# The opening's four tiles by seven products in the first feed-forward block's down product

## The chip, the cores and the metric

The kernel runs on one core of a Trainium2 chip. Times are microseconds (us) of device time for one execution. TensorE (PE in the profile) multiplies matrices, VectorE (DVE) and ScalarE (ACT) do elementwise work and read the products out of PSUM, GpSimd (POOL) and SyncE (SP) here mostly issue transfers (DMA). Each engine works through its own list of instructions in the list's order and waits on semaphores for the others.

## The reference

Two layers of an encoder over 640 rows (512 prompt rows and 8 streams of 16 rows), width 1024. Each layer is a half-step feed-forward block, a mixer (short convolution and banded attention, joined by gates), and a second half-step feed-forward block. All is float32. The part that the change touches is the first block:

```python
x = x + 0.5 * swiglu(rmsnorm(x, norm_ffn1), w_gu, w_down)     # D_MODEL 1024, D_FF 2816

def _swiglu(h, w_gu, w_down):
    gu = h @ w_gu
    g, u = jnp.split(gu, 2, axis=-1)
    return (jax.nn.silu(g) * u) @ w_down
```

## The kernel before

**Layout.** The activations are held transposed, features on the 128 partitions and the 640 rows along the free axis, so x is 8 tiles of 128x640 and the hidden layer is 22 tiles (`FT`). Each float32 operand is split into a high part (ScalarE casts it, lines 221 and 307) and a low part (VectorE subtracts, lines 222 and 312), and each product is three matmuls: high by high, high by low, low by high. One matmul streams 320 columns, half of a tile's rows.

**Two ways to multiply.** A plain product of two tiles (`multiply`, line 370) takes 6 matmuls: three for each half of the rows. The other way (`block`, line 391) takes two neighbouring tiles of weights, two of the inner dimension and the two halves of the rows as a 2x2 block product and needs 7 products where the plain way needs 8. The operands are then sums and differences, of the weights and of the activations, named `X11`, `XT5`, `XN6`, `X21`, `XT7`, `X22`, `XT4` for the seven products; the results are put together by further additions.

**Units and chunks.** `gate_up` makes one hidden tile: its u and its g by seven products, 84 matmuls over four slabs of prepared weights (`s0` to `s3`). One call of it is called a unit here. The hidden tiles are worked in chunks of `FFNS`, for the first block of layer 0 ("a0") 4, 4, 4, 4, 4 and 2. The first four tiles of "a0" are the opening: they are multiplied the plain way (`opening`, line 604) while the normalisation is still being worked out. While a chunk's units run, the chunk before is multiplied with the down weights and added to x. For a chunk that is made by seven (`by_seven`), that is two calls of `down_rows`, after the second and the third unit (`ROWS`), each over four rows of output tiles: seven products of 12 matmuls over four slabs, with x updated from PSUM by VectorE (`take`), or by staging a product through ScalarE (`stage`) into an accumulating DMA that POOL issues (`send`). For other chunks it is one slab of 8 plain tiles behind each unit (two output tiles, 48 matmuls). In "a0" the four tiles of the opening go the plain way, behind units 4, 5, 6 and 7.

**Weights.** `source` loads the raw weights (SP's queue, three buffers and a fourth) and forms their sums on VectorE (line 251: two of 512 columns for slab 1, two for slab 2); `prep` casts the high part on ScalarE and `flush` emits the low part on VectorE. There are three buffers for prepared slabs; one is read by TensorE and two lie ahead. A by-seven unit or call has slabs of 1024, 1024, 1024 and 512 columns.

**Pairs.** Two hidden tiles of a chunk form a `Pair`. Its first tile gives E (the product of g and u, a difference of its halves, and the cast and low part for `X11` and `XT5`); its second gives O (`X21`, `X22`) and, in five steps of `rest`, three combinations (lines 911 and 913), their cast and low part (`XN6`, `XT7`), and a cast and low part of 320 columns (`XT4`, here called t4). E and O have one buffer each. The steps are run at named spots of later units, by `TURNS`.

**Order.** `manual_schedule` keeps the order in which the code emits instructions. In "a0" it holds for PE, DVE and ACT until unit 6 (`free`), and from there for PE alone. What closes a unit (g by the norm, the product of g and u, the pair's part) is a `tail`, which the code runs in what follows: in the slab of the down product, at spot e1 of the next unit, or in a call of `down_rows`. A unit's three PSUM banks a, b and c are copied or added out between the products (lines 820, 833, 836 copy a and c; in unit 4, which comes first, lines 767, 777 and 786); a bank that was copied takes the next product on top, so that product waits for the copy. Four such banks go round.

**The opening's tiles.** Their tails, `parts(2)`, `parts(3)`, `parts(0)`, `parts(1)`, each a cast and a low part of 640 columns, run inside unit 4, two after its first product and two after its fourth.

Of the kernel before, what the change touches and what calls it, by code (L numbers as in the profile page):

```python
# [13 lines left out]
ALU = mybir.AluOpType  # L14
# [17 lines left out]
FT = FF // P  # L32
# [45 lines left out]
def by_seven(name, j):  # L78

    at, n = chunk_at(name, j)  # L80
    return n == 4 and at >= FFNS[name][1] and at + n < FT


def ffn_order(name):
# [93 lines left out]
def halves(t):  # L178
    return t.rearrange("p (a b) -> p a b", a=2)
# [3 lines left out]
def trunk(ctx: ExitStack, tc: tile.TileContext, xin, wst, small, pbias, samplebias, kcache, vcache,  # L183
          yout, ko, vo, co):
    nc = tc.nc
    PE, DVE, ACT, POOL, SP = nc.tensor, nc.vector, nc.scalar, nc.gpsimd, nc.sync
# [33 lines left out]
    def split(hi, lo, src):  # L220
        ACT.copy(hi, src)
        DVE.tensor_tensor(out=lo, in0=src, in1=hi.bitcast(F32), op=ALU.subtract)
# [87 lines left out]
    def flush():  # L310
        for lo, src, hi in pending:
            DVE.tensor_tensor(out=lo, in0=src, in1=hi.bitcast(F32), op=ALU.subtract)  # L312
        pending.clear()
# [16 lines left out]
    def ahead():  # L330

        source(len(ready))

    def begin():

        prep(used[0] + 2)
# [264 lines left out]
            ACT.activation(early, epst, AF.Silu)  # L601
            self.known = True

    def opening(fp, name, goff, n, put, tails):

        ACT.copy(early, epst)
        ex = Expand(fp, name, goff)
        h = []  # L610
        whi, wlo = (wp.tile([P, CH], F32R, tag=f"w{t}", name=f"w{t}0", bufs=3) for t in ("hi", "lo"))
        ready.append((whi, wlo))
        for k in range(KT):
            g = sm[:, goff + k : goff + k + 1]
            hi = hp.tile([P, T], F32R, tag="hhi", name=f"hhi{name}_{k}")
            lo = hp.tile([P, T], F32R, tag="hlo", name=f"hlo{name}_{k}")
            ACT.activation(hi, x[k], AF.Copy, scale=g)
            c = slice(k * P, (k + 2) * P)
            if k % 2 == 0:
                ACT.copy(whi[:, c], raws[0][:, c])  # L620
            DVE.scalar_tensor_tensor(out=lo, in0=x[k], scalar=g, in1=hi.bitcast(F32),
                                     op0=ALU.mult, op1=ALU.subtract)
            if k % 2 == 0:
                DVE.tensor_tensor(out=wlo[:, c], in0=raws[0][:, c], in1=whi[:, c].bitcast(F32),
                                  op=ALU.subtract)
            h.append((hi, lo))
        flush()

        made = {2: (0, 1), 3: (2, 3), 4: (4,), 5: (5, 6), 6: (7,)}
        us, gs, ps = [], [], []  # L630

        def out(i):

            j, up = divmod(i, 2)
            if not up:
                gs.append(tmp(f"g{name}_{j}"))
                if j:
                    scaled(gs[j], ps[i], ex.rho)
                    ACT.activation(gs[j], gs[j], AF.Silu)
                else:  # L640
                    ACT.copy(halves(gs[j]), two(ps[i]))
                return
            u = tmp(f"u{name}_{j}") if j > 1 else fp.tile([P, T], F32, tag="cap", name=f"u{name}_{j}", bufs=5)
            us.append(u)
            if j:
                scaled(u, ps[i], ex.rho)
                DVE.tensor_tensor(out=u, in0=u, in1=gs[j], op=ALU.mult)
            else:
                ACT.copy(halves(u), two(ps[i]))

        def begun():
            ex.total(att(f"nps{name}"))
            ex.root()
            ex.diagonal()

        at = {2: {4: begun}, 3: {1: lambda: ex.spread([att(f"nbc{name}_{a}")[:, :HT] for a in range(2)])}}
        for i in range(2 * n):
            ps.append(acc(f"po{name}_{i}"))
            product(ps[i], h, at.get(i, {}))
            if i > 1:  # L660
                out(i - 1)
            if i == 0:
                for k in range(KT):
                    ex.square(k)
                    ex.add()
                    if k == 1:
                        out(0)
                    if k == 4:
                        flush()
            if i == 1:  # L670
                continue
            if i == 3:
                g, u = gs[0], us[0]
                DVE.tensor_tensor(out=g, in0=g, in1=ex.rho, op=ALU.mult)
                ACT.activation(g, g, AF.Silu)
                DVE.tensor_tensor(out=u, in0=u, in1=ex.rho, op=ALU.mult)
            flush()
            for m in made.get(i, ()):
                ex.final(m, False)
            if i == 3:  # L680
                DVE.tensor_tensor(out=u, in0=u, in1=g, op=ALU.mult)
            if i == max(made):
                ex.rest()
        ahead()
        begin()
        out(2 * n - 1)

        def parts(j, u):
            hi = hp.tile([P, T], F32R, tag="hhi", name=f"ahi{name}_{j}")
            lo = hp.tile([P, T], F32R, tag="hlo", name=f"alo{name}_{j}")  # L690
            split(hi, lo, u)
            put(j, (hi, lo))


        for j in sorted(range(n), key=lambda j: j < 2):
            tails.append(lambda j=j: parts(j, us[j]))
        ex.rest = None
        return ex

# [40 lines left out]
        with soon():  # L740
            last(pa)

    def gate_up(fp, n, ex, first, tails, put, j, pair, later, at):

        pa, pb, pc = (att(f"p{i}{n}")[:, :HT] for i in "abc")

# [5 lines left out]

        def spot(name):
            step(later, f"g{at}{name}")

        every, most, end = range(NP), range(NP - 1), range(NP - 1, NP)
        g, u = tmp(f"g{n}"), tmp(f"u{n}")
# [59 lines left out]
        else:  # L817
# [3 lines left out]
            prep(used[0] + 1)  # L821
            spot("e1")
            for t in tails:
                t()
            tails.clear()
            spot("e2")
            flush()
# [21 lines left out]
        DVE.tensor_tensor(out=g[:, t1], in0=pa, in1=rho[:, t1], op=ALU.mult)  # L849
        ACT.activation(g, g, AF.Silu, scale=-1.0)  # L850
        spot("e7")
        flush()

        def tail(weights=True):
            if weights:
                begin()
            DVE.tensor_tensor(out=g, in0=g, in1=rho, op=ALU.mult)
            hi = hp.tile([P, T], F32R, tag="hhi", name=f"ahi{n}")
            lo = hp.tile([P, T], F32R, tag="hlo", name=f"alo{n}")
            if pair:  # L860
                pair.product(n, u, g, hi, lo)
            else:
                DVE.tensor_tensor(out=u, in0=u, in1=g, op=ALU.mult)
                flush()
                split(hi, lo, u)
            put(j, (hi, lo))
            if weights:
                ahead()

        tails.append(tail)  # L870

    class Pair:
# [8 lines left out]
        def product(self, n, u, g, hi, lo):  # L881
            if self.E is None:

                z = self.E = self.fp.tile([P, 3, HT], F32, name=f"de{n}", tag="even", bufs=1)
                DVE.tensor_tensor(out=z[:, 0:3:2], in0=halves(u), in1=halves(g), op=ALU.mult)
                DVE.tensor_tensor(out=z[:, 1], in0=z[:, 0], in1=z[:, 2], op=ALU.subtract)
                at, kinds = slice(0, 2), (X11, XT5)
            else:

                z = self.O = self.fp.tile([P, 5, HT], F32, name=f"do{n}", tag="odd", bufs=1)  # L890
                DVE.tensor_tensor(out=z[:, 3:5], in0=halves(u), in1=halves(g), op=ALU.mult)
                at, kinds = slice(3, 5), (X21, X22)
                self.later.append(self)
                self.work = self.rest()
            flush()
            ACT.copy(halves(hi), z[:, at])
            self.low(halves(lo), halves(hi), z[:, at])
            self.keep(kinds, hi, lo)

        def low(self, lo, hi, z):  # L900
            DVE.tensor_tensor(out=lo, in0=z, in1=hi.bitcast(F32), op=ALU.subtract)
# [27 lines left out]
    def step(later, place):  # L929

        for p in later:
            while p.done < 5 and p.spots[p.done] == place:
                next(p.work)
                p.done += 1
# [83 lines left out]
    def ffn(name, fp, ex, goff, after, end=False):  # L1018
# [7 lines left out]
        hold[0] = True  # L1026

        mode = ExitStack()
        free = min(j for j in range(FT) if by_seven(name, j)) + 2

        def order(engines):
            mode.close()
# [1 line left out]

        order(ORDERED)
        if plain:
            ex = opening(fp, name, goff, plain, act.__setitem__, tails)
        for what, a in ffn_order(name):
            if what == "gu" and a == free:
                order({mybir.EngineType.PE})  # L1040
# [4 lines left out]
            if what == "gu":  # L1045
                pair = None
                if by_seven(name, a):
                    i, odd = divmod(a - chunk_at(name, a)[0], 2)
                    if not odd:
                        at = chunk_at(name, a)[0]  # L1050
                        rows = at and by_seven(name, at - 1)
                        pairs[a] = Pair(fp, f"{name}_{a}", i, later, TURNS[i if rows else i + 2])
                    pair = pairs[a - odd]
                gate_up(fp, f"{name}_{a}", ex, a == plain, tails, act.__setitem__, a, pair, later,
                        a - chunk_at(name, a)[0])
                continue
            if what == "rows":
                ms, js = a
# [827 lines left out]
```

## Time and profile before

| | |
|---|---|
| median of 3 runs | 2522.73 us (2522.15 to 2523.34) |
| profiled execution | 2522.74 us |
| its span in the profile | 2521.0 us |
| TensorE busy | 2502.0 us, 17192 matmuls |
| VectorE busy | 2117.7 us |
| ScalarE busy | 1325.1 us |
| unit 4 begins | 67.06 us |
| unit 7's down slab ends | 144.50 us |

A row of a timeline begins with the start and the duration of an instruction; then come the engine, the line of the code, what is written and read, and, in brackets, how long the engine stood idle before it and what ended that. A row of a window gives each engine's busy time, with its number of instructions, then the granted clock, the share of the DMA engines that was busy, and their rate. In a list of waits stand the engine and line that waited, whom for, the total, how often, and the longest. TensorE's matmuls overlap, so their rate is read from one start to the next.

### The profile page before, as it was taken

How to read it: one execution, taken by the hardware profiler on the slowest of the kernel's cores; microseconds unless marked ns; L12 is line 12 of the kernel's file. 1: busy time of each engine (PE TensorE's matmuls, PEld its weight loads, DVE VectorE, ACT ScalarE, POOL GpSimd, SP SyncE). 2: the span in 40 equal slices, each digit the busy share in tenths (PEclk: the TensorE clock that was granted, in tenths of full speed). 3: DMA queues.
4: the chain of work that ended last, by engine and by line, in shares of the span. 5: the costliest groups of instructions: out<-in, count | busy, mean ns of one | idle time of the engine just before them, and what ended most of it. 6: DMA issues, size and time to landing. Idle time of an engine off the chain costs nothing.

```text
span 2521.0 us, 42929 instructions
## 1 busy us (share of the span) xinstructions
PE 2502.0 (99%) x17192; PEld 2441.3 (97%) x17192; DVE 2117.7 (84%) x3347; ACT 1325.1 (53%) x2084; POOL 185.6 (7%) x249
## 2 busy tenths in 40 slices
PE   9999999999999999999999999999999999999998
PEld 9999999888999999999999999998889999999998
DVE  7889888878677899988699999888786768899997
ACT  7445556664444545555455555557644455455553
POOL 0000112111000001000001000021110000010000
PEclk9999999999999999999999999999999999999999
DMA  4233444334222234343224343443342222243434
GB/s 144 76 105 103 115 115 126 107 114 162 76 85 92 75 101 115 105 110 100 84 76 112 110 116 100 115 118 124 129 138 84 76 93 76 86 114 109 123 100 99
DMA packets 99320, 265.40 MB, mean 105 GB/s; under 512 B 9680, under 2 KB 45136, under 8 KB 99120
## 3 DMA queue, kind: packets, MB, share of 16 engines
q1 hardware_dynamic: 69408, 220.76, 26.7%
q0 software_dynamic: 28992, 41.26, 9.3%
q8 instruction: 135, 2.21, 0.4%
q10 hardware_dynamic: 720, 0.65, 0.1%
q14 instruction: 65, 0.53, 0.1%
HBM read 222.70 MB, written 7.94 MB: 91 GB/s over the span
## 4 chain that ended last, share of the span: by engine, by line
PE 92%; ACT 4%; DVE 3%; issue 1%; DMA 0%; DVEq 0%; ACTq 0%
PE pab L397 12%; PE paa L397 11%; PE pcb L397 6%; PE pca L397 6%; PE daa L952 5%; PE py L374 4%; PE po L374 4%; PE qa L397 4%; PE pdb L374 4%; PE dab L952 4%; PE pbb L397 3%; PE pba L397 3%; PE poa L374 2%; PE pda L374 2%; PE pv L1392 2%; PE ma_cv L397 2%
## 5 line engine op out<-in xcount | busy, mean ns | idle before, releaser
L312 DVE TENSOR_TENSOR wlo<-raw,whi 128x1024 fp32r<-128x1024 f32 (+1 forms) x566 | 585.6, 1037 | 177.8 <-ACT whi L307 172.6
L307 ACT CAST whi<-raw 128x1024 fp32r<-128x1024 f32 (+1 forms) x566 | 509.1, 903 | 366.6 <-PE pbb L397 38.6
L307 ACT CAST whi<-s 128x1024 fp32r<-128x1024 f32 (+1 forms) x152 | 144.4, 950 | 279.5 <-issue 89.3
L397 PE MATMUL pab<-xhib,whi 128*128 128x320 f32 x704 | 218.1, 310 | 0.3
L397 PE MATMUL pab<-xhib,wlo 128*128 128x320 f32 x704 | 217.3, 309 | 0.0
L397 PE MATMUL pab<-xlob,whi 128*128 128x320 f32 x704 | 217.2, 309 | 0.0
L397 PE MATMUL paa<-xhia,whi 128*128 128x320 f32 x640 | 198.0, 309 | 1.0 <-ACT c_a L833 0.6
L397 PE MATMUL paa<-xhia,wlo 128*128 128x320 f32 x640 | 197.5, 309 | 0.0
L397 PE MATMUL paa<-xloa,whi 128*128 128x320 f32 x640 | 197.5, 309 | 0.0
L312 DVE TENSOR_TENSOR wlo<-s,whi 128x1024 fp32r<-128x1024 f32 (+1 forms) x152 | 166.3, 1094 | 9.8 <-ACT whi L307 9.8
L397 PEld LDWEIGHTS pab<-xhib,whi 128*128 128x128 f32 x704 | 132.1, 188 | 0.9 <-ACT c_b L833 0.8
L397 PEld LDWEIGHTS pab<-xlob,whi 128*128 128x128 f32 x704 | 132.1, 188 | 0.2
L397 PEld LDWEIGHTS pab<-xhib,wlo 128*128 128x128 f32 x704 | 132.1, 188 | 0.0
L397 PEld LDWEIGHTS paa<-xhia,whi 128*128 128x128 f32 x640 | 120.1, 188 | 1.6 <-ACT c_a L833 0.9
L397 PEld LDWEIGHTS paa<-xloa,whi 128*128 128x128 f32 x640 | 120.1, 188 | 0.1
L397 PEld LDWEIGHTS paa<-xhia,wlo 128*128 128x128 f32 x640 | 120.1, 188 | 0.0
L976 POOL DMA_DIRECT2D x<-c_b x28 | 33.8, 1209 | 1105.6 <-ACT c_b L969 457.8
L397 PE MATMUL pcb<-xhib,wlo 128*128 128x320 f32 x352 | 108.8, 309 | 0.0
L397 PE MATMUL pcb<-xlob,whi 128*128 128x320 f32 x352 | 108.6, 309 | 0.0
L397 PE MATMUL pcb<-xhib,whi 128*128 128x320 f32 x352 | 108.6, 309 | 0.0
L976 POOL DMA_DIRECT2D x<-c_a x36 | 43.6, 1212 | 865.1 <-ACT whi L307 386.4
L251 DVE TENSOR_TENSOR raw<-raw,raw 128x512 f32<-128x512 f32 x152 | 103.7, 683 | 0.8
(681 smaller groups left out, 7943.2 us busy)
## 6 DMA issues: line engine op xcount, KB each, us to landing
raw<-in_wst SPq DMA_DIRECT2D x378, 512.0 KB, 3.5
x<-c_a POOLq DMA_DIRECT2D x36, 320.0 KB, 4.2
x<-c_b POOLq DMA_DIRECT2D x28, 320.0 KB, 4.1
kc<-in_kcache SPq DMA_DIRECT2D x32, 256.0 KB, 3.8
vc<-in_vcache SPq DMA_DIRECT2D x16, 512.0 KB, 4.7
x<-u_a POOLq DMA_DIRECT2D x18, 320.0 KB, 5.4
x<-u_b POOLq DMA_DIRECT2D x14, 320.0 KB, 5.5
bias<-in_pbias POOLq DMA_DIRECT2D x16, 256.0 KB, 3.6
```

The lines of the kernel that those rows point to most:

```text
L251: DVE.tensor_tensor(out=out, in0=a, in1=b, op=ALU.add)
L307: ACT.copy(hi[:, d], src[:, c])
L312: DVE.tensor_tensor(out=lo, in0=src, in1=hi.bitcast(F32), op=ALU.subtract)
L374: PE.matmul(ps[:, a, :HT], w, x[:, a * HT : (a + 1) * HT], start=first and j == 0, stop=last and j == 2)
L397: PE.matmul(ps, a, b, start=start and kp == 0 and j == 0, stop=stop and kp == NP - 1 and j == 2, skip_group_check=True)
L952: PE.matmul(ps[u], w, y, start=start and i == 0 and j == 0, stop=i == 1 and j == 2, skip_group_check=True)
L976: POOL.dma_start(rows(r, cols), z, accum_op=ALU.add)
L1392: PE.matmul(pv[t], xx[:, t * P : (t + 1) * P], w[:, kk * AW : (kk + 1) * AW], start=c == 0 and kk == 0 and j == 0, stop=c == KT // 2 - 1 a ...
```

## The change

The four tiles of the opening are multiplied with the down weights by seven as well: two pairs (0 and 2), and two calls of `down_rows` behind units 5 and 6 in place of the four plain slabs behind units 4, 5, 6 and 7. The weights are laid out for it by the same functions on the host.

The tiles u of the opening already hold the product of g and u, so `Pair.product` gets no g and copies the tile with ScalarE. The work of the two pairs is written out by hand over units 4 and 5: in unit 4 pair 2's E and O after the first product and its three combinations, cast and low part after the fourth; in unit 5 its t4 and pair 0's E at spot e1, pair 0's O at e2, its five steps at e3, e4 and e7.

E and O have one buffer each, so pair 4 can begin only behind pair 0. Unit 4's tail is split: in unit 5 it only prepares weights at e1, and its `finish` (g by the norm, E of pair 4) is run at the end of unit 5, before the last `flush`. Unit 5's tail runs in the first call. Since the chunk before it now goes by seven, chunk 4 to 7 takes the other half of `TURNS`: pair 4's combinations stand in the first call (r0d1) and its other steps in unit 7; pair 6's stand in units 8 and 9. The order stays free from unit 6 on, as before.

```diff
 def by_seven(name, j):
     at, n = chunk_at(name, j)
-    return n == 4 and at >= FFNS[name][1] and at + n < FT
+    return n == 4 and at + n < FT
...
-        def parts(j, u):
+        def parts(j):
             hi = hp.tile([P, T], F32R, tag="hhi", name=f"ahi{name}_{j}")
             lo = hp.tile([P, T], F32R, tag="hlo", name=f"alo{name}_{j}")
-            split(hi, lo, u)
+            pairs[j - j % 2].product(f"{name}_{j}", us[j], None, hi, lo)
             put(j, (hi, lo))
-        for j in sorted(range(n), key=lambda j: j < 2):
-            tails.append(lambda j=j: parts(j, us[j]))
+        for i in range(n // 2):
+            pairs[2 * i] = Pair(fp, f"{name}_{2 * i}", i, later, ())
+        def rest(i, n):
+            for _ in range(n):
+                next(pairs[2 * i].work)
+        tails += [lambda: parts(2), lambda: parts(3), lambda: rest(1, 3)]
+        extra.update({"e1": lambda: (rest(1, 2), parts(0)), "e2": lambda: parts(1), "e3": lambda: rest(0, 2),
+                      "e4": lambda: rest(0, 2), "e7": lambda: rest(0, 1)})
...
         def spot(name):
             step(later, f"g{at}{name}")
+            if extra:
+                extra[name]()
...
             spot("e1")
             for t in tails:
-                t()
+                t(main=not extra)
+            held = tails[:]
             tails.clear()
...
         spot("e7")
+        if extra:
+            for t in held:
+                t(False)
         flush()
-        def tail(weights=True):
+        def tail(weights=True, main=True):
             if weights:
                 begin()
+            if main:
+                finish()
+            if weights:
+                ahead()
+        def finish():
             DVE.tensor_tensor(out=g, in0=g, in1=rho, op=ALU.mult)
...
             put(j, (hi, lo))
-            if weights:
-                ahead()
...
-                DVE.tensor_tensor(out=z[:, 0:3:2], in0=halves(u), in1=halves(g), op=ALU.mult)
+                self.times(z[:, 0:3:2], u, g)
...
+        def times(self, out, u, g):
+            if g is None:
+                ACT.copy(out, halves(u))
+            else:
+                DVE.tensor_tensor(out=out, in0=halves(u), in1=halves(g), op=ALU.mult)
...
-        free = min(j for j in range(FT) if by_seven(name, j)) + 2
+        free = min(j for j in range(plain, FT) if by_seven(name, j)) + 2
...
                 gate_up(fp, f"{name}_{a}", ex, a == plain, tails, act.__setitem__, a, pair, later,
-                        a - chunk_at(name, a)[0])
+                        a - chunk_at(name, a)[0], extra if plain and a == plain + 1 else None)
```

More of the change, by code (lines that the diff above doesn't have):

```diff
@@ L602, in spread, with opening @@
             self.known = True
-    def opening(fp, name, goff, n, put, tails):
+    def opening(fp, name, goff, n, put, tails, extra, pairs, later):
         ACT.copy(early, epst)
@@ L741, in seven, with gate_up @@
             last(pa)
-    def gate_up(fp, n, ex, first, tails, put, j, pair, later, at):
+    def gate_up(fp, n, ex, first, tails, put, j, pair, later, at, extra=None):
         pa, pb, pc = (att(f"p{i}{n}")[:, :HT] for i in "abc")
@@ L890, in product @@
                 z = self.O = self.fp.tile([P, 5, HT], F32, name=f"do{n}", tag="odd", bufs=1)
-                DVE.tensor_tensor(out=z[:, 3:5], in0=halves(u), in1=halves(g), op=ALU.mult)
+                self.times(z[:, 3:5], u, g)
                 at, kinds = slice(3, 5), (X21, X22)
-                self.later.append(self)
+                if self.spots:
+                    self.later.append(self)
                 self.work = self.rest()
@@ L1036, in ffn @@
         if plain:
-            ex = opening(fp, name, goff, plain, act.__setitem__, tails)
+            extra = {}
+            ex = opening(fp, name, goff, plain, act.__setitem__, tails, extra, pairs, later)
         for what, a in ffn_order(name):
```

## The prediction

> **What bounds the kernel now.** I read the page's head and first part, then TensorE's list of waits, the windows view over the stretch that the change touches, and last the timelines of the three engines there.
>
> ```profile
> span 2521.0 us, 42929 instructions
> PE 2502.0 (99%) x17192; PEld 2441.3 (97%) x17192; DVE 2117.7 (84%) x3347; ACT 1325.1 (53%) x2084; POOL 185.6 (7%) x249
> ```
> ```profile
> PE poa L374 <- ACT whi L620: 5.9, 1, 5.9
> ...
> PE paa L397 <- ACT c_a L833: 0.6, 1, 0.6
> ...
> PE paa L397 <- ACT c_a L820: 0.3, 1, 0.3
> ```
>
> TensorE hardly ever waits: 5.9 us for the first weights, then fractions. The profiled execution took 2522.74 us, against a median of 2522.73, so 1.74 us lie outside its span, and I add to 2522.74.
>
> ```profile
> core 0: us, PE busy (x) PEld busy (x) DVE busy (x) ACT busy (x) POOL busy (x), PEclk, DMA share, GB/s
> 67.06:79.38 12.32, 12.32 (x86) 12.32 (x85) 10.39 (x16) 7.16 (x11) 0.00 (x0) 1.00 0.25 82
> 79.38:86.42 7.04, 7.04 (x50) 7.04 (x49) 6.80 (x10) 2.52 (x3) 0.00 (x0) 1.00 0.26 83
> 86.42:98.75 12.33, 12.33 (x87) 12.33 (x85) 8.18 (x14) 4.85 (x7) 0.00 (x0) 1.00 0.30 89
> 67.06:144.50 77.44, 77.44 (x530) 77.44 (x529) 64.27 (x94) 32.72 (x47) 0.00 (x0) 1.00 0.25 82
> 144.50:230.00 85.50, 85.38 (x582) 85.11 (x581) 75.47 (x115) 43.78 (x64) 7.44 (x6) 1.00 0.42 110
> ```
>
> The rows are unit 4, its down slab, unit 5, all of units 4 to 7 with their four slabs, and a stretch whose down work already goes by seven. A unit's 84 matmuls fill 12.32 us and a slab's 48 fill 7.04: one every 0.147 us. VectorE carries 83% of the whole stretch.
>
> **The change, part by part.** *TensorE.* The opening's down product is 8 x 4 tiles by 6 matmuls, 192; by seven it is two calls of 7 products by 12, 168. So 24 x 0.147 = **3.5 us less**, all on the path.
>
> *Prices*, start to start where instructions stand back to back (a row's end overlaps the next start by some 0.1):
>
> ```profile
> 69.85 1.22 DVE L312 TENSOR_TENSOR wlo<-raw,whi 128x1024 fp32r<-128x1024 f32 x1
> 70.98 1.55 DVE L222 TENSOR_TENSOR aloa<-ua,ahia 128x640 fp32r<-128x640 f32 x2
> 74.30 0.49 DVE L251 TENSOR_TENSOR ua<-pba,c_a 128x320 f32<-128x320 f32 x1 [1.77 <-PE pba L397]
> ...
> 81.12 0.68 DVE L251 TENSOR_TENSOR s<-raw 128x512 f32<-128x512 f32 x1
> 81.84 0.69 DVE L251 TENSOR_TENSOR s<-s,raw 128x512 f32<-128x512 f32 x1
> 82.45 0.82 DVE L857 TENSOR_TENSOR ga<-ga,rhoa 128x640 f32<-128x640 f32 x1
> 83.30 0.82 DVE L885 TENSOR_TENSOR dea<-ua,ga 128x640 f32<-128x640 f32 x1
> 84.16 0.49 DVE L886 TENSOR_TENSOR dea<-dea 128x320 f32<-128x320 f32 x1
> 84.57 1.22 DVE L312 TENSOR_TENSOR wlo<-s,whi 128x1024 fp32r<-128x1024 f32 x1
> ...
> 87.65 1.55 DVE L1088 SCALAR_TENSOR_TENSOR x<-pda,x 128x640 f32<-128x640 f32 x2
> ...
> 108.10 0.48 DVE L911 SCALAR_TENSOR_TENSOR doa<-dea,doa 128x320 f32<-128x320 f32 x1
> ```
> ```profile
> 69.31 0.42 ACT L767 COPY c_a<-paa 128x320 f32<-128x320 f32 x1
> 69.62 1.36 ACT L221 CAST ahia<-ua 128x640 fp32r<-128x640 f32 x2
> ...
> 72.54 0.42 ACT L786 COPY c_a<-paa 128x320 f32<-128x320 f32 x1 [1.23 <-PE paa L397]
> ...
> 88.71 1.05 ACT L307 CAST whi<-raw 128x1024 fp32r<-128x1024 f32 x1
> 90.05 0.63 ACT L307 CAST whi<-raw 128x512 fp32r<-128x512 f32 x1 [0.28 <-ACT whi L307]
> ...
> 110.18 0.46 ACT L923 CAST t4hia<-doa 128x320 fp32r<-128x320 f32 x1
> ...
> 171.13 0.71 ACT L966 ACTIVATE c_a<-daa 128x640 f32<-128x640 f32 x1
> ```
>
> VectorE: 1.14 for 1024 columns, 0.74 for 640, 0.60 for 512, 0.40 for 320; ScalarE 0.95, 0.63, 0.53, 0.32. An instruction that needs another engine's result starts 0.04 after that one ends.
>
> *Weights.* Four plain slabs become two by-seven groups. VectorE: 4 x 1.14 = 4.6 goes, 2 x (3 x 1.14 + 0.60 + four sums of 0.60 to 0.72) = 13.1 comes: +8.5. ScalarE +3.0. The number of raw loads stays four.
>
> *Opening's pairs.* Four low parts go (3.0); each of two pairs gets a difference, two low parts, three combinations, a 640 and a 320 low part (4.3): VectorE +5.6. ScalarE gets per pair two copies and three casts of 640 and one of 320, less four splits: +4.5.
>
> *x.* Eight updates of 0.74 become two sets of three of 0.74 and two of 0.40: nothing. ScalarE stages 2 x 3 tiles: +3.9.
> ```profile
> raw<-in_wst SPq DMA_DIRECT2D x378, 512.0 KB, 3.5
> x<-c_a POOLq DMA_DIRECT2D x36, 320.0 KB, 4.2
> ```
>
> *Queues.* SP issues the same raw loads, and each waits for its buffer: the call's second one for unit 4's last low part (ending 78.4 in the walk below), landing 3.5 later at 82, wanted at 97. I take nothing; a load late by more than 15 would be seen. POOL gets six accumulating DMAs, 4.2 to landing; the stretch 144.50 to 230.00 has such ones (POOL works 7.44 us) and TensorE idles 0.12 in it. I take nothing; a late one would hold a staging buffer, of which there are five.
>
> So VectorE needs about 64.3 + 14.2 = 78.5 us in a stretch that shrinks to 77.4 - 3.5 = 73.9. What doesn't fit can lag into the next stretch (10.0 us free), but weights have only two slabs of lead, so I walked the written order (units 4, 5 and the first call are in manual order on all three engines) with the prices above.
>
> *Unit 4.* Until 70.98 nothing changes. Then VectorE and ScalarE hand pair 2 to and fro: difference to 71.47, cast to 72.24, low part at 72.28. ScalarE, behind two casts and two copies, makes the copy of line 786 at 73.86 instead of 72.54, ending 74.28; the next product into that bank is due at 74.10: **0.2**. VectorE adds at 74.41, forms three combinations to 76.21, waits for their cast (76.98), makes their low part and the fourth slab's, and reads bank a at 78.35 to 78.84; the product due at 77.84 waits **1.0**. No idle 1.8 us is left at 72.5, and no down slab follows in which VectorE could catch up: the 7.04 us moved behind unit 5.
>
> *Unit 5* starts at 80.64. VectorE is still at unit 4's end (its last read of bank a ends 82.61; bank b of unit 5 is that buffer: **0.2**), the low part of slab 1 runs at 83.33, the raw sums end 85.75. Only then ScalarE can cast slab 2 (85.79), and behind this stand the t4 cast, two copies, two casts of pair 0 and slab 3, with a wait for VectorE's difference between; line 833's copy runs at 90.94 to 91.37. TensorE wants that bank at 87.92: **3.5**. The next copy (line 836) stands behind pair 0's three combinations and their cast, ending 94.71 against 93.17: **1.6**.
>
> *First call.* Unit 4's held tail stands at unit 5's end, ahead of slab 1's low part and, through the cast of E, ahead of the staging copy. VectorE gets through t4's low part, g x rho, E, the difference at 103.03; the low part ends 104.25, the staging copy 104.53, due 101.79: **2.8**, and **0.3** later in the call. All seven make 9.6.
>
> The same wait stands in this trace, smaller, where layer 1's first unit runs its tail inside the second:
>
> ```profile
> 1284.61 0.49 DVE L886 TENSOR_TENSOR dea<-dea 128x320 f32<-128x320 f32 x1
> ...
> 1285.14 0.73 ACT L896 CAST ahia<-dea 128x640 fp32r<-128x640 f32 x1 [0.50 <-DVE dea L886]
> 1285.77 0.42 ACT L833 COPY c_a<-paa 128x320 f32<-128x320 f32 x1
> ...
> 1286.24 0.41 PE L397 MATMUL paa<-xhia,whi 128*128 128x320 f32 x1 [0.65 <-ACT c_a L833]
> ```
>
> There one cast of E ahead of line 833's copy costs 0.65; here four casts and two copies stand there. Written order is kept even where a later copy was ready. [...]
>
> *After the first call* order is free for VectorE and ScalarE. Kept in written order, unit 6 would wait 0.75 more; the stretch from 144.50 shows 0.12 in 85.5. I take 0.2, nearest to that row, and keep 0 and 0.75 (and 2, if the second call also waits) for the range.
>
> **Sum.** -3.5 + 9.6 + 0.2 = +6.3: 2522.74 + 6.3 = **2529.0 us**, 0.25% more.
>
> **The rivals.** *The work hides (other side).* ScalarE's own work between lines 820 and 833 in unit 5 is 0.95 + 4 x 0.63 + 0.53 + 0.36 = 4.4; from the first product's result (unit start + 2.0) with both 320 copies it ends at +7.1, and TensorE wants it at +7.04. So if VectorE reached slab 2's sums within some 1 us of the unit's start, the two waits of 5.1 would vanish, the others shrink under 3.5, and the time would fall, at best to 2522.74 - 3.5 = 2519.2. It decides at waits of 3.5 in all. For it: 4.15 idle us of VectorE in unit 5 before (12.33 less 8.18). Against: these sums end 5.1 us after the unit's start in the walk. 0.12.
>
> *Partly.* Only VectorE's own sum counts: from 69.85 to the first call's second low part six instructions of 1.14, eight of 0.74, ten of 512 columns (6.2) and 21 of 0.40, together 27.4 us, so it ends at 97.3. TensorE without waits wants it at 67.06 + 2 x 12.32 + two products of 1.76 + two matmuls, 95.5: 1.8 of wait. With some of the hand-overs up to 8: 2521.0 to 2527.2. For it: the durations alone give this much; against it: the row at 1286.24, where a hand-over cost what its order says. 0.18.
>
> *The lag doesn't drain.* In the walk VectorE ends the first call's work 3.4 us after TensorE. Two units (8.7 each: four weight sums 2.5, four low parts 4.0, five of 0.40), a call (9.6), a tail of E (2.9) and pair 4's two low parts (1.1) follow, with the 3.4 some 34.4 us for TensorE's 37.0. If waits there take 2 to 4 us: 2531 to 2533. Against: the row of 144.50 to 230.00. 0.10.
>
> *The clock drops.* TensorE ran slow after its first idle time:
>
> ```profile
> 5.86 0.90 PE L374 MATMUL poa<-hhia,whi 128*128 128x320 f32 x2 [5.86 <-ACT whi L620]
> ...
> 10.91 0.72 PE L374 MATMUL poa<-hhia,whi 128*128 128x320 f32 x2
> 11.45 0.49 PE L374 MATMUL poa<-hloa,whi 128*128 128x320 f32 x2
> ```
>
> 20 matmuls took 5.6 us there instead of 2.9. If the wait of 3.5 us does this again, 2.7 are lost: 2531.7. Against: no idle time inside this trace is over 1.0, so nothing shows it mid-run. 0.08. [...]
>
> **How the numbers follow.** Forecast 0.52 (waits of 8 to 11: 2527.2 to 2530.7), partly 0.18, hides 0.12, lag 0.10, clock 0.08. The range 2522.5 to 2532.0 leaves out hiding and the upper ends. 0.2% is 5.05 us, about what can be told from no change: slower starts at 2527.8, inside the forecast's own range, so slower is 0.87 of 0.52 plus lag and clock, 0.63; faster would need 2517.7, below all that is saved, 0.02; same 0.35.
>
> **What would show it.** Right: TensorE 17168 matmuls; waits on the copies of lines 786, 833, 836 and the staging copy between 74 and 112 us, some 9 us in all; VectorE over 95% busy there; the old 1.77 gap gone. Wrong: none of these rows, with unit 6's first product 3.5 us earlier than 24 matmuls allow for; or matmul pitch above 0.147 after the longest wait.

## The result, and the profile after

The changed kernel takes 2530.77 us (median of 7 runs, 2530.13 to 2531.54), the kernel before beside it 2522.71 (2521.9 to 2523.8): a ratio of 1.0033, 95% interval 1.0023 to 1.0043. It is slower, by 8.1 us where 6.3 were forecast, inside the range.

Head and first line of the page of the changed kernel:

```profile
span 2529.2 us, 42953 instructions
...
PE 2502.3 (99%) x17168; PEld 2439.6 (96%) x17168; DVE 2131.3 (84%) x3373; ACT 1336.9 (53%) x2104; POOL 192.8 (8%) x255
```

The 24 matmuls are gone, and the span is 8.2 us longer. TensorE's waits between 66 and 156 us (the new code is some 25 lines longer: line 843 was 833, 846 was 836, 990 is the staging copy, formerly 966):

```profile
PE paa L397 <- ACT c_a L843: 3.3, 1, 3.3
PE daa L976 <- ACT c_a L990: 2.4, 1, 2.4
PE paa L397 <- DVE ga L251: 0.9, 1, 0.9
```

Before, no wait of TensorE is listed in this stretch. Measured from start to start, the three are 3.5, 2.6 and 1.0. The chain ahead of the longest, on ScalarE's timeline:

```profile
85.84 1.05 ACT L307 CAST whi<-raw 128x1024 fp32r<-128x1024 f32 x1 [1.60 <-DVE raw L251]
...
88.44 0.72 ACT L914 CAST ahia<-dea 128x640 fp32r<-128x640 f32 x1 [0.56 <-DVE dea L903]
...
90.34 0.72 ACT L914 CAST ahia<-doa 128x640 fp32r<-128x640 f32 x1
90.97 0.42 ACT L843 COPY c_a<-paa 128x320 f32<-128x320 f32 x1
```

The cast of slab 2 starts late because VectorE's sums are late, E's cast waits for VectorE's difference, and the copy that TensorE needs stands behind all of it at 90.97. That copy was forecast for 90.94.

What was not in the forecast's sum stands in the windows of 2 us each behind the two long waits:

```profile
core 0: us, PE busy (x) PEld busy (x) DVE busy (x) ACT busy (x) POOL busy (x), PEclk, DMA share, GB/s
90.00:92.00 2.00, 0.56 (x2) 0.56 (x3) 1.78 (x4) 1.36 (x3) 0.00 (x0) 0.90 0.69 195
92.00:94.00 2.00, 2.00 (x9) 2.00 (x9) 1.61 (x4) 0.32 (x1) 0.00 (x0) 0.50 0.86 274
...
106.00:108.00 2.00, 2.00 (x10) 2.00 (x9) 2.00 (x3) 1.04 (x2) 0.00 (x0) 0.50 0.00 0
```

The granted clock fell to a half, twice, for 3.4 us each: from 91.6 to 95.0 and from 105.2 to 108.7. Both falls stand behind idle time of TensorE, the waits of 3.5 and 2.6 us.

VectorE was busy 32.8 of the 38.0 us from 74 to 112, 86%; the prediction's sign for being right was over 95%.

From the start of unit 4 to the start of unit 8 the chunk takes 85.65 us in place of 77.44, 8.2 more, so nearly all of the loss lies here: units 4 and 5 lose 6.9 (waits 4.8 start to start, half clock 1.8, small gaps 0.3), the first call 4.2 (wait 2.6, half clock 1.6), units 6 and 7 with the second call 0.6, and 3.5 are saved.

### The profile page after: what moved, and what is told of

The parts are those of the page before. It is cut to its first block, busy times and chain, and to the rows that moved or that the text cites. A ratio compares the mean times of both kernels' runs of the same rounds, so it can differ in the third digit from the quotient of the medians.

```text
span 2529.2 us, 42953 instructions
## 1 busy us (share of the span) xinstructions
PE 2502.3 (99%) x17168; PEld 2439.6 (96%) x17168; DVE 2131.3 (84%) x3373; ACT 1336.9 (53%) x2104; POOL 192.8 (8%) x255
## 4 chain that ended last, share of the span: by engine, by line
PE 88%; DVE 5%; ACT 4%; issue 1%; DMA 0%; SPq 0%; DVEq 0%; ACTq 0%
PE pab L397 12%; PE paa L397 10%; PE pcb L397 6%; PE pca L397 5%; PE daa L976 5%; PE py L374 4%; PE po L374 4%; PE qa L397 4%; PE pdb L374 4%; PE dab L976 4%; PE pbb L397 3%; PE pba L397 3%; PE pv L1417 2%; PE dca L976 2%; PE ma_cv L397 2%; PE ma_qk L397 2%
## 5 line engine op out<-in xcount | busy, mean ns | idle before, releaser
L312 DVE TENSOR_TENSOR wlo<-raw,whi 128x1024 fp32r<-128x1024 f32 (+2 forms) x568 | 586.6, 1036 | 174.6 <-ACT whi L307 169.3
L307 ACT CAST whi<-raw 128x1024 fp32r<-128x1024 f32 (+2 forms) x568 | 510.2, 902 | 357.3 <-PE pbb L397 38.4
```

Of the source, the lines that this page charges most:

```text
L307: ACT.copy(hi[:, d], src[:, c])
```

## The experiments

The first theory was the forecast's: VectorE and ScalarE have more work than fits ahead of the first call (load), so that moving steps only moves the waits. Its rival: the work fits, and the order in which it is written on two engines that feed each other makes the waits (order). Where `manual_schedule` does not hold an engine's instructions, the tool that builds the program orders them by itself; it is called the planner here. A third question was what the half clock costs by itself. Medians are compared with the kernel before, run beside each group: 2522.68 us for the first four, 2522.58, 2522.48 and 2522.93 for the next groups of four, three and one.

**TensorE kept busy in the first call's wait.** The product ahead of the wait is computed twice.

```diff
         mul(b, s0, 1, X21, True)
+        if n.startswith("a0_0_0"):
+            mul(b, s0, 1, X21, True)
         take(B, 0, t1)
```

> The changed kernel with the first call's second product (12 matmuls, 1.76 us) computed twice, so that TensorE has work inside the 2.6 us that it waits for the staging copy; nothing else moves. Clock theory (the wait itself makes TensorE run at half clock for the 3.4 us behind it, which costs 1.65): the wait falls to about 0.8, the pitch behind it stays at 0.147 us, and 12 more matmuls make the kernel 1.6 us faster than the change, about 2529.1 us. Rival (the clock falls there for another reason, or the slow stretch hides work that was late anyway): no change in time, 2530.8 us, or 1.7 more if the wait isn't free.

Measured: 2530.52 us (2530.16 to 2531.42), 7.8 above before, not told apart from the change, as the rival had it. TensorE's waits between 66 and 156 us:

```profile
PE paa L397 <- ACT c_a L843: 3.4, 1, 3.4
PE paa L397 <- DVE ga L251: 0.9, 1, 0.9
PE paa L397 <- DVE wlo L312: 0.8, 1, 0.8
PE daa L976 <- ACT c_a L990: 0.5, 1, 0.5
```

and the window that had half clock:

```profile
106.00:108.00 2.00, 2.00 (x15) 2.00 (x15) 1.97 (x4) 1.32 (x3) 0.00 (x0) 1.00 0.00 0
```

The clock stays up, 15 matmuls in 2 us instead of 10, so the wait did cause the fall. But the 1.65 us don't come out in the time: TensorE gets ahead and then waits 0.8 for unit 6's low part (line 312), which it had hardly waited for while it ran slow. The half clock was in good part paid with time that TensorE would have waited anyway.

**Both waits filled.** As above, and the product ahead of the wait in unit 5 is computed three times.

```diff
             spot("e3")
             mul(pc, s1, 1, XT5, every, True, True)
+            if extra:
+                mul(pc, s1, 1, XT5, every, True, True)
+                mul(pc, s1, 1, XT5, every, True, True)
```

> As the kernel before it, and in unit 5 the XT5 product is computed three times (3.5 us more of TensorE's work inside the wait for the copy of line 843). Theory: the slow stretch behind that wait goes too, but the next product then waits some 1.5 us for the copy of line 846, which ends at 94.7 us in either case, so the time stays at about 2529.1 us. Rival (each slow stretch adds its own 1.6 us): 2527.5 us.

Measured: 2531.04 us (2530.77 to 2531.85), 8.4 above before. The clock is 1.00 from 67 to 152 us, and the next product now waits 1.3 us for the copy behind, as expected; but the time was expected to fall by 1.6 us, and none is gained from the clock.

**One step moved behind the copy.**

```diff
-"e2": lambda: parts(1), "e3": lambda: rest(0, 2),
+"e2": lambda: None, "e3": lambda: (parts(1), rest(0, 2)),
```

> The changed kernel with pair 0's O moved from spot e2 to spot e3, behind the copy of line 843 on ScalarE. Load theory (VectorE and ScalarE together have more to do by the first call than fits, and order only decides where TensorE waits for it): the wait on line 843 falls from 3.4 to 2.1 and the wait on line 846 rises to 2.9; total waits the same, 2530.8 us within 1. Order theory (the copy's place in ScalarE's queue is the cause): at least 1.3 us less and up to 3.4, 2527.4 to 2529.5 us.

Measured: 2530.79 us (2530.0 to 2531.65), 8.1 above before. Its waits:

```profile
PE pca L397 <- ACT c_a L846: 2.3, 1, 2.3
PE paa L397 <- ACT c_a L843: 2.0, 1, 2.0
```

The wait is split in two, half clock lasts some 6.7 us from 91.4 on (a clock of 0.85 in 90 to 92, 0.83 in 79.4 to 99, 1.00 behind that), as long in sum as in the change, and nothing is gained, as the load theory had it; that it also fits a written order in which the next step is just as badly placed showed only later.

**The pairs' work left out.** Each tile of the opening is only split into its high and its low part, and these stand for all seven operands: the kernel leaves out the sums and differences that the seven products need.

```diff
-            pairs[j - j % 2].product(f"{name}_{j}", us[j], None, hi, lo)
+            split(hi, lo, us[j])
             put(j, (hi, lo))
+            kinds = ((X21, X22), (XT4,)) if j % 2 else ((X11, XT5), (XN6, XT7))
+            for k in kinds:
+                pairs[j - j % 2].keep(k, hi, lo)
...
-        tails += [lambda: parts(2), lambda: parts(3), lambda: rest(1, 3)]
+        tails += [lambda: parts(2), lambda: parts(3), lambda: parts(0), lambda: parts(1)]
```

> The pairs' work is left out: the opening's four tiles are split as before the change, inside unit 4, and the seven products read these splits as operands, so the sums and differences of the activations and their casts and low parts are not computed; the weights, the calls and the place of unit 4's tail stay as changed. Load theory: no wait in units 4 and 5; the wait before the first call's third product stays at 2.2 to 2.5, since it comes from unit 4's tail; -3.5 + 2.4 + 0.5 makes 2522.1 us, and 2523.7 us if that wait alone still halves the clock. Rival (the three more slabs' casts, sums and low parts don't fit, pairs or not): above 2527 us.

Measured: 2523.77 us (2522.93 to 2524.14), a ratio of 1.0004 (0.9995 to 1.0012). Waits:

```profile
PE daa L978 <- ACT c_a L992: 2.1, 1, 2.1
PE paa L397 <- DVE wlo L312: 1.1, 1, 1.1
```

The waits of units 4 and 5 are gone, the one before the first call's third product stays, as it comes from unit 4's tail. The clock did not fall behind the wait of 2.1: it is 1.00 from 67 to 152 us. In the written order the pairs' work costs 7.0 us of the change; the weights, calls and tail use up the 3.5 that are saved and 1.1 more. This kernel has less work and other queues at once, so it does not tell load from order.

**The planner from unit 5 on**, and, after its result, **from unit 4 on**. The work is the same; only the order of VectorE and ScalarE is no longer the written one.

```diff
-        free = min(j for j in range(plain, FT) if by_seven(name, j)) + 2
+        free = 5 if plain else min(j for j in range(plain, FT) if by_seven(name, j)) + 2
```

> The changed kernel with the written order of VectorE and ScalarE given up one unit earlier: from unit 5 on, instead of from unit 6 on, the planner orders them; the work is the same. Load theory (the work doesn't fit before the first call, so order moves the waits and takes away only the part that is hand-over): 1 to 4 us less than the change, 2526.8 to 2529.8 us. Order theory (the written order alone causes the waits of unit 5 and the first call, some 6 us): 2524 to 2525 us.

Measured: 2524.98 us (2524.7 to 2525.8), 2.4 above before: 5.7 us of the change's loss are gone, more than the load theory allowed, and as the order theory had it.

```diff
+        free = 4 if plain else min(j for j in range(plain, FT) if by_seven(name, j)) + 2
```

> The changed kernel with the order of VectorE and ScalarE left to the planner from unit 4 on (the run before left it from unit 5 on, 2524.98 us). Load theory: VectorE is busy all the time from unit 5 to the first call already, so the 1.0 us that unit 4 waits comes back later; within 1 us of that run, 2524.0 to 2525.5 us. Order theory: the 1.3 us of unit 4 and most of what is left go, 2522 to 2523 us.

Measured: 2521.76 us (2521.41 to 2522.63), 0.7 below before, a ratio of 0.9997 (0.9989 to 1.0006). Both theories missed it, load by more. The same work (3373 instructions of VectorE, 2104 of ScalarE in both) takes 8.8 us less in the planner's order than in the written one. **The load theory falls**: the work fits without the waits. Unit 4 in the change (first fence), then units 4 and 5 in this kernel, by windows:

```profile
67.06:79.38 12.32, 11.39 (x76) 10.91 (x75) 9.99 (x17) 6.94 (x11) 0.00 (x0) 1.00 0.15 44
```
```profile
67.00:79.40 12.40, 12.40 (x87) 12.40 (x86) 12.40 (x21) 7.54 (x12) 0.00 (x0) 1.00 0.26 86
79.40:99.00 19.60, 19.11 (x131) 18.85 (x130) 19.60 (x32) 12.76 (x20) 0.00 (x0) 1.00 0.19 54
```

VectorE (the third busy time) works without a gap, 12.40 of 12.40 and 19.60 of 19.60, where the written order left it 10.0 of 12.3, waiting for ScalarE's casts.

**The low parts on POOL.** Only the opening's pairs have empty `spots`, so only their eight low parts move.

```diff
-            DVE.tensor_tensor(out=lo, in0=z, in1=hi.bitcast(F32), op=ALU.subtract)
+            (DVE if self.spots else POOL).tensor_tensor(out=lo, in0=z, in1=hi.bitcast(F32), op=ALU.subtract)
```

> The changed kernel with the low parts of the opening's two pairs (six of 640 columns, two of 320, 5.2 us of VectorE) made by POOL; ScalarE's work and the written order stay. By the queues in written order: the wait on line 843 stays at 3.4, since what stands ahead of it on ScalarE waits for VectorE's difference and sums and not for low parts; the wait behind it and that of the first call shrink; 2.5 us less than the change, 2528.3 us. Rival (VectorE's summed work alone sets the waits): 5 us less, 2525.6 us. If POOL slows VectorE down while both read SBUF: 2530 us or more.

Measured: 2533.09 us (2532.82 to 2533.74), 10.5 above before: 2.4 slower than the change, though VectorE has eight instructions less; this is the third case expected. The wait on line 843 stays, at 3.5. POOL's timeline, and VectorE's at the same time:

```profile
74.34 1.56 POOL L925 TENSOR_TENSOR aloa<-doa,ahia 128x640 fp32r<-128x640 f32 x1
...
91.14 1.70 POOL L925 TENSOR_TENSOR aloa<-dea,ahia 128x640 fp32r<-128x640 f32 x1 [1.18 <-ACT ahia L914]
```
```profile
74.79 0.49 DVE L251 TENSOR_TENSOR ua<-pba,c_a 128x320 f32<-128x320 f32 x1 [2.83 <-PE pba L397]
75.19 1.06 DVE L935 SCALAR_TENSOR_TENSOR doa<-dea,doa 128x320 f32<-128x320 f32 x1
76.29 0.49 DVE L935 SCALAR_TENSOR_TENSOR doa<-doa 128x320 f32<-128x320 f32 x1
...
91.62 1.77 DVE L312 TENSOR_TENSOR wlo<-raw,whi 128x512 fp32r<-128x512 f32 x1 [0.18 <-ACT whi L307]
```

VectorE's instructions that read from SBUF alone (the chip's memory for tiles outside PSUM) and began while POOL worked did not end before POOL's had: 1.06 instead of 0.48, ending 0.35 us after POOL's, and 1.77 instead of 0.68 for 512 columns, ending 0.55 after. The one at 74.79, which reads a product from PSUM, took its usual 0.49 beside the same POOL instruction. POOL needed 1.6 us for what VectorE does in 0.82, and seven of the eight moved held VectorE up instead of relieving it.

**Another written order.** Pair 0's E, O and casts stand behind the copies that free a bank; unit 4's and unit 5's tails and pair 4's combinations stand inside the first call, behind its staging copies. The steps are made one by one at the named places (`a` to `d` in unit 4, `e1` to `e7` in unit 5, `r0` to `r6` in the call; A and B are E's copy with its difference and E's cast with its low part, C and D the same for O, R1 to R5 the steps of `rest`, the last digit is the pair; F4 and F5 the two tails, G4 the combinations).

```diff
+        plan = {"a": ("A2", "B2", "C2", "D2"), "b": ("R12",), "d": ("R22",), "e1": ("R32", "R42"),
+                "e3": ("R52", "A0"), "e4": ("B0", "C0"), "e5": ("D0", "R10", "R20"),
+                "e7": ("R30", "R40", "R50"), "r2": ("F4",), "r5": ("F5",), "r6": ("G4",)}
```

> The same work as the change in another written order: in units 4 and 5 the steps of pairs 2 and 0 stand behind the copies that free a bank (pair 0's E from spot e3 on, its O after unit 5's third slab, its casts before the first call), and unit 4's tail, unit 5's tail and pair 4's combinations stand inside the first call, behind the staging copies. Load theory: the waits on lines 843 and 846 go, and one of some 3 us comes in the first call, with 1 to 2 more behind it; together 4 us less than the change, 2526.7 us, still above before. Rival (order alone): all waits go, 2520 to 2522 us. Rival (waits only move): 2530.8 us.

Measured: 2526.19 us (2525.21 to 2527.15), 3.6 above before, 4.5 less than the change, where the load theory expected 4 and the order theory 9 to 11. The waits that are left, the first being the forecast one in the call:

```profile
PE daa L1005 <- ACT c_a L1023: 2.1, 1, 2.1
PE daa L1005 <- DVE wlo L312: 0.5, 1, 0.5
```

Half clock follows them: the pitch is 0.27 from 100.67 on, and the clock over 99 to 116 us is 0.90. So a hand-written order can be better or worse by 4 us with the same work. By its figure alone this run speaks for load; what decides against it is the planner's order from unit 4 on, and the best version below.

**The other order with POOL's low parts.** The plan one spot earlier for pair 0 (E's copy in unit 4, its casts at e3), the low parts as above.

```diff
+        plan = {"a": ("A2", "B2", "C2", "D2", "R12"), "b": ("R22", "R32", "R42", "R52", "A0"),
+                "e3": ("B0", "C0", "D0", "R10"), "e5": ("R20",), "e6": ("R30",),
+                "r1": ("R40", "R50"), "r2": ("F4",), "r5": ("F5", "G4")}
```

> As the kernel before it, with pair 0's steps one spot earlier again and the opening pairs' low parts on POOL. If load and order both count: 7 us less than the change, 2523.9 us, and down to 2521 us where the planner does better behind unit 5 than the written order. If POOL disturbs VectorE: no better than the kernel before it.

Measured: 2532.22 us (2531.17 to 2532.75), 9.6 above before and 6.0 worse than that other order alone, the third case of what was expected. But the plan differs in some steps too, so how much of the 6.0 is POOL's is not separated.

**Both cures together**, the other written order, and the planner from unit 5 on.

```diff
+        free = 5 if plain else min(j for j in range(plain, FT) if by_seven(name, j)) + 2
```

> The spread written order (tails and pair 4's combinations inside the first call) with the planner's order from unit 5 on. Load theory: what is left after the planner is VectorE's work that doesn't fit, so about the planner's time again, 2524 to 2525.5 us. Rival (the two cures add up): 2521 to 2522.5 us, at or below the kernel before.

Measured: 2521.29 us (2521.03 to 2522.06), 1.2 below before, a ratio of 0.9995 (0.9986 to 1.0004): the cures add up but for 0.9 us (4.5 and 5.7 alone, 9.3 together).

**The planner, without the pairs' work** (the two edits above together).

> Both at once: the sums, differences, casts and low parts of the opening's pairs are left out (the products read plain splits), and the planner orders VectorE and ScalarE from unit 5 on. Load theory: with 5.6 us of VectorE's and 4.5 us of ScalarE's work gone and the tail's hand-over free, the 24 matmuls' 3.5 us come through: 2519.2 to 2520.2 us. If the weights' and calls' work alone is too much: 2522 us or more.

Measured: 2520.75 us (2519.98 to 2521.51), 1.7 below before. TensorE lists no wait between 60 and 430 us, and the mixer behind the block starts 2.4 us earlier than before (428.7 against 431.1). About 0.7 are lost again by the end. So even with no pair's work at all the saving that reaches the end is about half of 3.5. From 67 to 143 us TensorE's starts fall back by 0.8 us in three places, each too short for the list; where the rest stays is open.

**The best version.** The other order and the planner from unit 4 on (`free = 4`, the plan as above).

> The spread written order with the planner's order from unit 4 on, the two cures that each came to 2521 to 2522 us. If what is left is the hand-over in units 4 and 5 (a wait of 0.8 us on the copy of u2 and one of 0.2 in the call): 0.5 to 1 us less, 2520.5 us. If it is VectorE's work that doesn't fit: 2521.3 us, the same as the spread order with the planner from unit 5 on.

Measured: 2520.31 us (2519.99 to 2521.64) against 2522.93, a ratio of **0.9990 (0.9981 to 0.9999)**: faster than the kernel before, and 10.7 us faster than the change by the differences to before, with the same work. It is also no slower than the kernel without the pairs' work above (2.6 below before, against 1.7), whose unit 4 is in written order: in a good order that work shows no cost. Its waits between 66 and 156 us, and its windows:

```profile
PE daa L1005 <- DVE x L1038: 0.5, 2, 0.2
...
79.40:99.00 19.60, 19.60 (x136) 19.60 (x135) 19.39 (x31) 12.10 (x19) 0.01 (x1) 1.00 0.21 67
```

and the copy that TensorE waited 3.4 us for (line 869 here):

```profile
86.00 0.42 ACT L869 COPY c_a<-paa 128x320 f32<-128x320 f32 x1
```

The copy runs at 86.0 instead of 91.0. VectorE is busy 19.39 of 19.60 us and TensorE 19.60.

## Why the prediction was right, and where its reason was not

*Saved: right.* 17168 matmuls at 0.147 us; 3.5 us.

*The walk through units 4 and 5 and the first call: right in nearly each row.* It is a walk of the written order, and as that it held. The waits on line 786 (795 now; 0.2 forecast, 0.2 in the trace), on bank a (1.0 and 1.0), on line 843 (3.5 and 3.5, start to start), in the first call (2.8 and 2.6) came where forecast; VectorE's difference for the held tail ended at 103.18, where the walk had it done at 103.03. The 0.2 on bank b of unit 5 did not come.

*The wait on line 846 (1.6): not seen as a wait.* The 12 matmuls ahead of it ran at half clock, 3.3 us instead of 1.76, and ended just as the copy did, at 94.7. That the slow clock cost no more than this wait is luck: two lengths that have nothing to do with each other came out the same. The sum is the same but for 0.2 at the next product.

*The clock: a rival with 0.08 came true, beside the forecast.* It was priced at 2.7 us after one wait; it came after two, for 1.8 and 1.6, and so one of the prediction's own signs of being wrong, a pitch above 0.147 behind the longest wait, came too. The first replaced the wait of 1.6. The second came on top of the sum and replaced its last 0.3: 1.3 more. With 0.4 more in units 4 and 5 (6.9 for 6.5), 0.4 more in units 6 and 7 than the 0.2 taken, and 0.2 less in the call's wait, this makes 1.9, against the 1.8 between forecast and result. The sum put the clock at nothing, and that is its largest miss. The two kernels with filled waits show that keeping the clock up gives next to none of it back (0.2 us less and 0.3 more than the change), since VectorE's list is late behind it.

*The reason given for it: wrong in one step.* "VectorE needs about 78.5 us in a stretch that shrinks to 73.9" is right as a sum: VectorE is busy 74.95 us between units 4 and 8 after the change, and 3.2 more than before fall into the stretch behind, where TensorE's waits did not grow. What does not follow is that TensorE must wait: in the best version as much lags into the stretch behind (78.66 us of VectorE, 75.47 before), and TensorE's listed waits are 0.5. The same work in the planner's order costs 8.8 us less, and with a better written start it beats the kernel before. The waits came from the order on two queues that feed each other, as the walk itself had priced them: VectorE idled for casts while ScalarE idled for sums, and each stood in order before work that TensorE needed. Two such gaps on VectorE's timeline of the changed kernel, in unit 5 where it is late already:

```profile
83.33 1.23 DVE L312 TENSOR_TENSOR wlo<-s,whi 128x1024 fp32r<-128x1024 f32 x1 [0.77 <-ACT whi L307]
...
87.28 0.49 DVE L925 TENSOR_TENSOR t4loa<-doa,t4hia 128x320 fp32r<-128x320 f32 x1 [1.53 <-ACT t4hia L947]
```

*Hiding (0.12): the mechanism is real, but not in this kernel.* It needed VectorE at slab 2's sums within 1 us of unit 5's start; they ended 5.0 us after it, at 85.75. In the best version the copy came 5 us earlier, and most of the price was gone.

*Partly:* its 1.8 us from VectorE's own sum are no floor, as the best version's 0.5 shows.

*The lag:* units 6 and 7 waited 0.6 in all, between the 0.2 taken and the bound of 0.75; the lag did drain.

## What to carry to other kernels

An instruction list walked by hand with the durations of the trace gave the waits of a fixed order to some 0.2 us here, and that is worth doing before writing such an order; but it prices the order, not the work. When two engines hand pieces to and fro, put ahead of each hand-over what a third engine is waiting for, in the whole order (one step moved alone gained nothing here), and ask what the planner would do with the same instructions before a step is held to be too much work. Removing one wait (or a slow clock behind it) shows little as long as the next wait in the same queues stands just behind it.

## What the runs showed of the hardware

- In the kernel whose low parts alone were moved, POOL's subtraction of two 128x640 float32 tiles took 1.55 to 1.76 us. The VectorE instructions begun meanwhile that read from SBUF alone did not end before it: 1.06 instead of 0.48 at 75.19, 1.77 instead of 0.68 at 91.62. Those that read a product from PSUM were not held up (0.49, 0.48 and 0.49 at 74.79, 93.31 and 97.20).
- In the changed kernel the granted clock was 1.00 from 9.67 to 91.59 us, 0.50 to 95.01, 1.00 to 105.24, 0.50 to 108.66, and 1.00 from there to 156. The falls came behind waits of TensorE of 3.5 and 2.6 us, and half clock lasted 3.4 us each time. With work put into both waits the clock was 1.00 from 67 to 152. The length of the wait alone did not decide it: a wait of 2.1 left the clock at 1.00 without the pairs' work, while in the other written order the pitch went to 0.27 behind one of 2.1 and another of 0.5 (ending at 99.30 and 100.36). What does decide it, these runs don't show.
- The slow start of the kernel before (20 matmuls in 5.6 us from 5.86 on) has a clock of 1.00 in its window. Its first record of the clock is at 11.5 us, just where the pitch falls to 0.147, so that column says nothing of the time ahead of it. The pitch there, 0.27 us, is that of the changed kernel at a clock of 0.50 (92.04 to 94.44), and is the safer sign of half clock.
